# A two-block transformer kernel: wide products issued first, one memory projection left in float32, and mixers without GpSimd arithmetic

## The chip, the cores and the metric

The kernel runs on one core of one Trainium2 chip. A core has a matrix engine (TensorE, PE in the rows; PEld is its weight load), a vector engine (VectorE, DVE), an activation engine (ScalarE, ACT), GpSimd (POOL), and SyncE (SP), which here issues the loads. The metric is the device time of one execution in microseconds (us); lower is better.

## The reference

Two blocks of two layers each over one sequence of 256 tokens, width 1024, all in float32. Cut to what matters here:

```python
# block 1
x = x + attn_conv_mixer(rms_norm(x), ...);  x = x + swiglu(rms_norm(x), w_gate, w_up, w_down)     # d_ff 3584
x = x + recurrent_mixer(rms_norm(x), ...);  x = x + moe_swiglu(rms_norm(x), router, ...)          # 8 experts, top 2
# block 2, for l in (0, 1)
x = x + 0.5 * swiglu_2(rms_norm_2(x), ffn1...)                                                    # d_ff 2816
z = rms_norm_2(x) @ mix_w_in[l]
x = x + concat(fox_mixer(z_fox), rwkv7_mixer(z_rwkv), moba_mixer(z_moba)) @ mix_w_out[l]
x = x + memory_cross_attention(rms_norm_2(x), rms_norm_2(mem), ...)
x = x + 0.5 * swiglu_2(rms_norm_2(x), ffn2...)

def memory_cross_attention(h, m, w_q, w_kv, q_gain, k_gain, w_o):
    kv = (m @ w_kv)                  # 256 x 1024 @ 1024 x 1024: first half keys, second half values
    k, v = rms_norm_2(kv keys, k_gain), kv values
    ...                              # the memory side does not depend on x

def rwkv7_mixer(...):                # per token t, 8 heads of 64
    state = state * w_t + sa * (kk_t * a_t) + v_t * k_t;  y_t = state @ r_t
```

## The kernel before

Tokens lie on 256 columns, features on 128 partitions; a wide product has 512 columns. Products that must keep float32 accuracy are split: each weight tile of 128 x 1024 is copied by ACT into a rounded high part `wh` (L192) and DVE subtracts it to get the low part `wl` (L193); the activations have a high and a low part too, `msh`/`msl` or the two halves of `hTa`/`hTb`. A product is then three matmuls, `mm3` at L204 to L206 (high by high, high by low, low by high).

The stages run in the order hybrid, ffn0, lru, moe, f1_0, mix_0, xa_0, f2_0, f1_1, mix_1, xa_1, f2_1. In an FFN, gate and up go through `proj_wide` (L396, L397): since the high and low halves of the normed activations lie side by side in `n.both`, one matmul of 512 columns does two of the three, and one of 256 columns does `wl` by high. Eight such pairs (k = 0 to 7) make one group in one bank of PSUM, two groups each for gate and up make a chunk. The down product (`acc`) uses L204 to L206 with 512 columns.

Weights arrive by SP's queue in tiles of 1 MB (`wt`) in a ring of `RING` = 6 buffers, which also holds the normed activations `hTa`, `hTb`. Small tiles of 128 x 512 come from `w4`, a set of buffers of its own for each "lane"; `SLOTS` gives their numbers. A lane is a generator whose steps are put between those of the main work: `fill` advances lane "f" or "g" by so many steps. The order on each engine is the one in which the code issues after these fills, moved a little by the scheduler.

In lru, lane "f" is `memory(0)`: it norms the memory, projects keys (`pmk`, split) and values (`pmv`, split), and evicts the values to `xv` (L1135, ACT). `memory(1)` runs in xa_0. At the end of lru the moe stage starts: it issues five expert tiles ahead (`AHEAD`), then `route`: router logits `plg` (L211), top 2 on DVE down to `r_M` (L850), ranks `prk` (L858), the largest count `mosti` (L868). Then every engine loads `mosti` (L1017, TENSOR_LOAD), takes a branch together (L1018), and goes on with the gather by one-hot products `pxg` (L911, its lists `oneh` from DVE, L899) and the experts.

In the mixers the rwkv part works on chunks of 64 tokens. `key` gives k and its norm; `be` (the tiles `a`, L1396) and `f` (tiles `kf`, L1397) are products of 128 x 512 on GpSimd. DVE runs the reciprocal square roots (`rsqrt`, steps at L294 to L303, of which the last spreads the result to 128 x 512, `kksq`). `gram` (L1490 to L1495) forms the matrices `gN`, `gB`, `gM` of the chunks: ACT copies them out of PSUM (L1490), GpSimd clears what lies above the diagonal in two pieces (L1495). From `gN` a triangular inverse is built in five levels, each a product `pX` (L1529), an eviction, a product `pY` (L1537), and two DVE steps (L1538, L1539); lanes fill in between. `moba` turns q and k with `rot` (L1225) on PE and two GpSimd products each (L1228, L1229).

Of the kernel before, what the change touches and what calls it, by code (L numbers as in the profile page):

```python
# [14 lines left out]
P = 128  # L15
# [3 lines left out]
SLOTS = {"":19,"f":11,"g":14}  # L19
# [15 lines left out]
class Norm:  # L35
# [3 lines left out]
    def __init__(self, K, x, gcol, raw=False):  # L39
        self.K, self.gcol, self.raw = K, gcol, raw  # L40
        self.xv = x if callable(x) else lambda b, lo, hi: x[:, b, lo:hi]
        self.hT, self.both = [], []
        self.ss = K.work.tile([P, 2, 2], FT, name="ss", tag="ss", bufs=2)

    def half(self, half):
# [6 lines left out]
        for kk in range(2):  # L52
            if self.raw:
                hf = K.w4("hTf")
                self.hT += [hf[:, k * S:(k + 1) * S] for k in range(2)]
            pt = K.ps("pt", tag="acc")
            for j in range(2):
                k = half * 4 + kk * 2 + j
                for b in range(2):
                    nc.tensor.transpose(pt[:, j * S + b * P:j * S + (b + 1) * P], xv(b, k * P, (k + 1) * P), K.ident)  # L60
            for j in range(2):
                k = half * 4 + kk * 2 + j
                o, g, t = pt[:, j * S:(j + 1) * S], self.gcol[:, k:k + 1], self.hT[k]
                if self.raw:
                    nc.vector.tensor_scalar(t, o, g, None, op0=OP.mult)
                    continue
                nc.scalar.activation(t[0], o, AF.Identity, scale=g)
                nc.vector.scalar_tensor_tensor(t[1], o, g, t[0].bitcast(FT), op0=OP.mult, op1=OP.subtract)
# [42 lines left out]
class Kern:  # L111
    def __init__(self, ctx, tc, a):
        self.tc, self.nc, self.a = tc, tc.nc, a
        self.lane = ""
        self.kv, self.aside = {}, {}
# [274 lines left out]
    def proj_wide(self, t, j, n, name, tag):  # L390


        mm, o = self.nc.tensor.matmul, slice(j * P, (j + 1) * P)
        p = self.ps(name, tag=tag)
        for k in range(KT):
            mm(p, t[k][0][:, o], n.both[k], start=k == 0, stop=False)  # L396
            mm(p[:, :S], t[k][1][:, o], n.hT[k][0], start=False, stop=k == KT - 1)  # L397
        return self.v2(p)
# [331 lines left out]
    def lru(self, x):  # L730
# [16 lines left out]
        self.aside = {"f": self.memory(0) if "mem_2" in a else None, "g": gates()}  # L747
# [261 lines left out]
    def moe(self, x):  # L1009
        gcol = self.colA["norm_ffn1"]  # L1010
        n = Norm(self, x, gcol, raw=True)
        yield n
        ahead = [self.wfetch(self.a[("moe_w_gate", "moe_w_up")[i // 2 % 2]][0, 0], i % 2 * 4, 4, i // 4 * 512, 512)
                 for i in range(AHEAD)]
        self.route(x, n)
        ahead[:SPLIT] = [self.wsplit(t, 4, 512) for t in ahead[:SPLIT]]
# [10 lines left out]
    def block2_setup(self):  # L1027
# [27 lines left out]
        for i in (0, 2):  # L1055
            nc.vector.tensor_scalar(self.mask3[:, i], self.jp, 0.0, NEG, op0=OP.is_gt, op1=OP.mult)

# [46 lines left out]
    def memory(self, l):  # L1104
# [32 lines left out]
        self.kv[l] = kn, vs  # L1137

# [70 lines left out]
    def softmax_heads(self, l, hT, rbc, c0, qg, kg, rope, bias=None, extra=None, sums=None):  # L1209
# [7 lines left out]
        for i, g in enumerate((g8, kg)):  # L1217
# [5 lines left out]
            if rope:  # L1223
# [4 lines left out]
                nc.gpsimd.tensor_tensor(self.v2(q1), self.v2(q1), self.bc2(self.cos), op=OP.mult)  # L1228
                nc.gpsimd.tensor_tensor(q1, q1, t, op=OP.add)  # L1229
# [80 lines left out]
    def rwkv(self, l, hT, rbc, plo, pk0, done):  # L1310
# [77 lines left out]
        for tp in range(2):  # L1388
# [7 lines left out]
            nc.gpsimd.tensor_tensor(be, be, Wi[tp], op=OP.mult)  # L1396
            nc.gpsimd.tensor_tensor(f, f, k, op=OP.mult)  # L1397
# [78 lines left out]
        def gram(lst, i, name, also=None, tag="acc", lane=""):  # L1476

            res = []
            for tp in range(2):
# [10 lines left out]
                nc.scalar.activation(g, p, AF.Copy)  # L1490
                if also:
                    also(tp, p)
                g8 = g.rearrange("p (n s) -> p n s", n=8)
                for rows, base in ((P, 64), (64, 0)):
                    nc.gpsimd.affine_select(out=g8[:rows], in_=g8[:rows], compare_op=OP.is_ge if i else OP.is_gt, fill=0.0,  # L1495
                                            base=base, pattern=[[0, 8], [1, 64]], channel_multiplier=-1)
# [289 lines left out]
```

## Time and profile before

| | us |
|---|---|
| three runs | 2804.93, 2807.41, 2796.13 (median 2804.93) |
| profiled execution, its own time | 2807.59 |
| its span | 2804.8 |
| PE busy | 2728.8 (97% of the span) |
| DVE busy | 2087.6 (74%) |
| ACT busy | 1688.5 (60%) |
| POOL busy | 72.0 (3%), 121 instructions |
| mean granted clock of TensorE | 0.982 |

Times of rows count from the start of the span. "Busy" of PE is a modelled overlap: matmuls start before the ones ahead end, so the distance from start to start tells what one costs in a stream, not its duration. The clock column is the granted TensorE clock as a share of full speed: 1.0 is 2.4 GHz, 0.5 is 1.2 GHz. A row of waits names the engine that stood idle, its line, and the instruction that released it.

### The profile page before, as it was taken

Reading aid. Unit: us, or ns where it says so; the run is one execution under the profiler, and the core shown is the slowest. Engines: PE = TensorE matmul, PEld = TensorE weight load, DVE = VectorE, ACT = ScalarE, POOL = GpSimd, SP = SyncE. Lnnn points to the kernel's source line nnn. Section 1 sums busy time; section 2 is a strip of 40 time slices with the busy share of each in tenths; the row PEclk is TensorE's granted clock in tenths of the full one; section 3 lists DMA queues with packets and bytes.
Section 4 is the critical chain, followed back from the end, with each engine's and each line's share of the span. In section 5 each row is a group of like instructions: output and inputs, shape, how many; then the busy total and the mean of one; then the engine's idle time right before and its main releaser. Section 6 shows DMA issues by size and latency. Waiting matters only on the chain. (4 is left out here: it accounts for less than half of the span.)

```text
span 2804.8 us, 46759 instructions
## 1 busy us (share of the span) xinstructions
PE 2728.8 (97%) x18959; PEld 2289.3 (82%) x18959; DVE 2087.6 (74%) x3041; ACT 1688.5 (60%) x2380; POOL 72.0 (3%) x121
## 2 busy tenths in 40 slices
PE   8999988999999999999999999999999999998999
PEld 7888886878787778778778888788888888787887
DVE  7767677988888888889887667557666666766665
ACT  5555565777777777777776556345555555544554
POOL 0010000000000000000000001010000000110000
PEclk9999998999999999999999999799999999899999
DMA  5555535999999989999996554123555555232453
GB/s 182 182 196 183 179 106 186 344 345 366 323 370 351 369 307 365 357 337 358 348 366 227 186 172 126 61 77 121 190 186 180 191 184 177 61 107 91 137 193 105
DMA packets 355711, 623.55 MB, mean 222 GB/s; under 512 B 12580, under 2 KB 187952, under 8 KB 355488
## 3 DMA queue, kind: packets, MB, share of 16 engines
q1 hardware_dynamic: 354448, 620.20, 63.8%
q8 instruction: 150, 2.46, 0.4%
q0 software_dynamic: 1040, 0.29, 0.1%
q14 instruction: 73, 0.60, 0.1%
HBM read 619.40 MB, written 1.05 MB: 221 GB/s over the span
## 5 line engine op out<-in xcount | busy, mean ns | idle before, releaser
L193 DVE TENSOR_TENSOR wl<-wt,wh 128x1024 fp32r<-128x1024 f32 x1176 | 1389.7, 1219 | 371.4 <-ACT wh L192 369.6
L192 ACT ACTIVATE wh<-wt 128x1024 fp32r<-128x1024 f32 x1176 | 1187.6, 1052 | 434.6 <-PE acc L206 92.3
L204 PE MATMUL acc<-wh,msh 128*128 128x512 f32 x544 | 214.0, 394 | 0.0
L206 PE MATMUL acc<-wh,msl 128*128 128x512 f32 x544 | 213.3, 392 | 0.0
L205 PE MATMUL acc<-wl,msh 128*128 128x512 f32 x544 | 212.4, 390 | 0.0
L205 PE MATMUL pu<-wl,xgh 128*128 128x512 f32 x448 | 179.1, 400 | 3.7 <-DVE wl L193 3.7
L204 PE MATMUL pg<-wh,xgh 128*128 128x512 f32 x448 | 176.7, 395 | 1.3 <-ACT xgh L918 1.3
L205 PE MATMUL pg<-wl,xgh 128*128 128x512 f32 x448 | 177.7, 397 | 0.0
L205 PE MATMUL ya<-wl,eh 128*128 128x512 f32 x448 | 177.4, 400 | 0.0
L204 PE MATMUL pu<-wh,xgh 128*128 128x512 f32 x448 | 175.5, 392 | 0.0
L206 PE MATMUL pg<-wh,xgl 128*128 128x512 f32 x448 | 175.3, 391 | 0.0
L206 PE MATMUL pu<-wh,xgl 128*128 128x512 f32 x448 | 175.3, 391 | 0.0
L206 PE MATMUL ya<-wh,el 128*128 128x512 f32 x448 | 174.1, 393 | 0.0
L204 PE MATMUL ya<-wh,eh 128*128 128x512 f32 x448 | 162.1, 392 | 0.0
L396 PE MATMUL pu<-hTa,wh 128*128 128x512 f32 x424 | 155.2, 399 | 0.3 <-DVE rbc L88 0.3
L396 PE MATMUL pu<-hTb,wh 128*128 128x512 f32 x424 | 154.9, 399 | 0.0
L396 PE MATMUL pg<-hTa,wh 128*128 128x512 f32 x424 | 154.7, 399 | 0.0
L396 PE MATMUL pg<-hTb,wh 128*128 128x512 f32 x424 | 154.3, 398 | 0.0
L206 PEld LDWEIGHTS acc<-wh,msl 128*128 128x128 f32 x544 | 102.2, 188 | 23.9 <-DVE msl L511 1.3
L204 PEld LDWEIGHTS acc<-wh,msh 128*128 128x128 f32 x544 | 102.2, 188 | 21.6
L397 PE MATMUL pu<-hTa,wl 128*128 128x256 f32 x424 | 119.2, 281 | 0.6 <-DVE wl L193 0.6
L397 PE MATMUL pu<-hTb,wl 128*128 128x256 f32 x424 | 119.6, 282 | 0.0
(702 smaller groups left out, 5604.8 us busy)
## 6 DMA issues: line engine op xcount, KB each, us to landing
wt<-in_moe_w_gate SPq DMA_DIRECT2D x112, 1024.0 KB, 7.1
wt<-in_moe_w_up SPq DMA_DIRECT2D x112, 1024.0 KB, 7.3
wt<-in_moe_w_down SPq DMA_DIRECT2D x112, 1024.0 KB, 6.3
wt<-in_ffn_w_in SPq DMA_DIRECT2D x88, 1024.0 KB, 5.2
wt<-in_ffn_w_out SPq DMA_DIRECT2D x44, 1024.0 KB, 5.1
wt<-in_mix_w_in SPq DMA_DIRECT2D x24, 1024.0 KB, 5.8
wt<-in_ffn_w_gate SPq DMA_DIRECT2D x14, 1024.0 KB, 5.0
wt<-in_ffn_w_up SPq DMA_DIRECT2D x14, 1024.0 KB, 5.1
```

The source lines that it names most:

```text
L192: i = nc.scalar.activation(h[:, m], t[:, s], AF.Copy)
L193: j = nc.vector.tensor_tensor(lo[:, m], t[:, s], h.bitcast(FT)[:, m], op=OP.subtract)
L204: nc.tensor.matmul(out, l[0], r[0], start=first, stop=False)
L205: nc.tensor.matmul(out, l[0], r[1], start=False, stop=False)
L206: nc.tensor.matmul(out, l[1], r[0], start=False, stop=last)
L396: mm(p, t[k][0][:, o], n.both[k], start=k == 0, stop=False)
L397: mm(p[:, :S], t[k][1][:, o], n.hT[k][0], start=False, stop=k == KT - 1)
```

## The change

Five things. `proj_wide` issues the eight wide matmuls of a group first, then the eight narrow ones. `memory(0)` in lru is replaced by `memory_keys(0)`, which leaves the normed memory in float32 in one tile of the weight ring (`memT`) and multiplies float32 weights unsplit: 32 matmuls of 256 columns for the keys; the values are left for `memory_values`, 16 matmuls of 512 columns on two weight tiles (`held`) that are fetched at the start of moe and used inside `route`'s stretch, before the branch. Three of five expert tiles are issued ahead of `route`, two behind the values. In both mixers `be`, `f` and the two rope products go from GpSimd to DVE. A gram leaves PSUM by one DVE operation, a bitwise and with a mask `chunk` that is made once; the ACT copy and the GpSimd pieces are gone. `SLOTS[""]` goes from 19 to 18.

```diff
-SLOTS = {"":19,"f":11,"g":14}
+SLOTS = {"":18,"f":11,"g":14}
@@ Norm
-                hf = K.w4("hTf")
+                i = (2 * half + kk) * 512
+                hf = K.w4("hTf") if self.home is None else self.home[:, i:i + 512]
@@ proj_wide
         for k in range(KT):
             mm(p, t[k][0][:, o], n.both[k], start=k == 0, stop=False)
+        for k in range(KT):
             mm(p[:, :S], t[k][1][:, o], n.hT[k][0], start=False, stop=k == KT - 1)
@@ lru
-        self.aside = {"f": self.memory(0) if "mem_2" in a else None, "g": gates()}
+        self.aside = {"f": self.memory_keys(0) if "mem_2" in a else None, "g": gates()}
@@ moe
+        held = self.held and [self.wfetch(self.a["xattn_w_kv_2"][self.held[0]], 4 * kh, 4, 512, 512) for kh in range(2)]
         yield n
...
+        ahead = first(AHEAD - 2)
         self.route(x, n)
+        if held:
+            with self.on("f"):
+                self.memory_values(held)
+        ahead += first(AHEAD - 2, AHEAD)
@@ block2_setup
+        self.chunk = c.tile([P, 2, 64], I32, name="chunk")
+        cm = self.w4("chm", P).rearrange("p (i s) -> p i s", i=2)
+        for i, op in enumerate((OP.is_gt, OP.is_ge)):
+            for h in (slice(0, 64), slice(64, P)):
+                nc.vector.tensor_scalar(cm[h, i], self.jp[h, h], 0.0, -1.0, op0=op, op1=OP.mult)
+        nc.vector.tensor_copy(self.chunk, cm)
@@ new: memory_keys (norm as in memory, raw, home = a ring tile), its products
+            t = self.wfetch(wkv, 0, KT, pr * 256, 256)
+            p = self.ps("pmk")
+            for j in range(2):
+                for k in range(KT):
+                    nc.tensor.matmul(p[:, j * S:(j + 1) * S], t[:, k * 256 + j * P:k * 256 + (j + 1) * P], n.hT[k],
+                                     start=k == 0, stop=k == KT - 1)
+                    if k % 2:
+                        yield
@@ new: memory_values
+        pv = [self.ps("pmv") for _ in range(2)]
+        for k in range(KT):
+            for b in range(2):
+                nc.tensor.matmul(pv[b], n.hT[k][:, b * P:(b + 1) * P], t[k // 4][:, k % 4 * 512:(k % 4 + 1) * 512],
+                                 start=k == 0, stop=k == KT - 1)
+        for b in range(2):
+            v = self.w4("xv")
+            nc.scalar.activation(v, pv[b], AF.Identity, scale=n.r[:, b:b + 1])
@@ rope
-                nc.gpsimd.tensor_tensor(self.v2(q1), self.v2(q1), self.bc2(self.cos), op=OP.mult)
-                nc.gpsimd.tensor_tensor(q1, q1, t, op=OP.add)
+                nc.vector.tensor_tensor(self.v2(q1), self.v2(q1), self.bc2(self.cos), op=OP.mult)
+                nc.vector.tensor_tensor(q1, q1, t, op=OP.add)
@@ rwkv
-            nc.gpsimd.tensor_tensor(be, be, Wi[tp], op=OP.mult)
-            nc.gpsimd.tensor_tensor(f, f, k, op=OP.mult)
+            V.tensor_tensor(be, be, Wi[tp], op=OP.mult)
+            V.tensor_tensor(f, f, k, op=OP.mult)
@@ gram
-                nc.scalar.activation(g, p, AF.Copy)
                 if also:
                     also(tp, p)
-                g8 = g.rearrange("p (n s) -> p n s", n=8)
-                for rows, base in ((P, 64), (64, 0)):
-                    nc.gpsimd.affine_select(out=g8[:rows], in_=g8[:rows], compare_op=OP.is_ge if i else OP.is_gt, fill=0.0,
-                                            base=base, pattern=[[0, 8], [1, 64]], channel_multiplier=-1)
+                bits = lambda t_: t_.bitcast(I32).rearrange("p (n s) -> p n s", n=8)
+                V.tensor_tensor(bits(g), bits(p), self.chunk[:, i:i + 1, :].to_broadcast([P, 8, 64]), op=OP.bitwise_and)
```

How the order moves at three places. First, PE from the last transposes of moe's norm (`pt`) to the branch, before:

```order
L211 MATMUL plg<-wr,hTf 32x8 x20
L60 MATMUL pt<-ident,x 128x128 x6
L211 MATMUL plg<-wr,hTf 32x8 x32
L858 MATMUL prk<-r_M,before 128x16
L858 MATMUL prk<-r_M,ones 128x16
L1017 TENSOR_LOAD mosti
L1018 COMPARE_AND_BRANCH
```

The same place of PE now, where lines count two or three higher, and L1194 is the matmul of `memory_values`:

```order
L213 MATMUL plg<-wr,hTf 32x8 x20
L1194 MATMUL pmv<-wt,memT 128x512
L62 MATMUL pt<-ident,x 128x128 x6
L1194 MATMUL pmv<-wt,memT 128x512
L213 MATMUL plg<-wr,hTf 32x8 x24
L1194 MATMUL pmv<-wt,memT 128x512
L213 MATMUL plg<-wr,hTf 32x8 x8
L1194 MATMUL pmv<-wt,memT 128x512 x5
L861 MATMUL prk<-r_M,before 128x16
L861 MATMUL prk<-r_M,ones 128x16
L1194 MATMUL pmv<-wt,memT 128x512 x8
L1029 TENSOR_LOAD mosti
```

Three of the sixteen stand ahead of the last router product, five ahead of `prk`, eight between `prk` and the load that the branch needs. On ACT, the activations at the same place, before:

```order
L875 ACTIVATE xsh<-x,rstd 128x512 x4
L845 ACT_TABLE_LOAD
L845 ACTIVATE r_e<-r_e 128x2
L1017 TENSOR_LOAD mosti
L1018 COMPARE_AND_BRANCH
```

And ACT now:

```order
L878 ACTIVATE xsh<-x,rstd 128x512 x4
L848 ACT_TABLE_LOAD
L848 ACTIVATE r_e<-r_e 128x2
L1199 ACTIVATE xv<-pmv,rstd 128x512 x2
L1029 TENSOR_LOAD mosti
L1030 COMPARE_AND_BRANCH
```

The two evictions of the values, which need all sixteen matmuls, have come ahead of ACT's own load and branch. Second, DVE in mixer 0, at the first of the two keys, before (`nwt`, `nwg` are the steps of a reciprocal square root, `wl` a weight split):

```order
L193 TENSOR_TENSOR wl<-wt,wh 128x1024
L298 TENSOR_TENSOR nwt<-nwt 128x8
L294 TENSOR_SCALAR nwg<-hn_t 128x8
L1269 COPY fz<-fz 4x256
L299 SCALAR_TENSOR_TENSOR nwt<-nwt,hn_t 128x8
L295 TENSOR_TENSOR nwg<-magic,nwg 128x8
L1407 TENSOR_TENSOR cum<-kf,cum 128x512
L303 SCALAR_TENSOR_TENSOR kksq<-nwt 128x512
```

DVE there now:

```order
L195 TENSOR_TENSOR wl<-wt,wh 128x1024
L300 TENSOR_TENSOR nwt<-nwt 128x8
L296 TENSOR_SCALAR nwg<-hn_t 128x8
L1461 TENSOR_TENSOR a_24269<-a_24269,cum 128x512
L301 SCALAR_TENSOR_TENSOR nwt<-nwt,hn_t 128x8
L297 TENSOR_TENSOR nwg<-magic,nwg 128x8
L1462 TENSOR_TENSOR kf<-kf,k 128x512
L305 SCALAR_TENSOR_TENSOR kksq<-nwt 128x512
L300 TENSOR_TENSOR nwt<-nwg 128x8
L1472 TENSOR_TENSOR cum<-kf,cum 128x512
```

`be` (L1461) and `f` (L1462) now stand on DVE ahead of the spread `kksq` that PE waits for, and the copy of `fz` and the product `cum` have gone behind it.

Third, PE in mixer 0 ahead of the inverse's first products, where the narrow matmuls `pv` of a lane stand between `gN` and `pX`. Before, `pX` came after 38 of them, of which these are the last:

```order
L597 MATMUL tm<-ident,av 128x128 x2
L205 MATMUL pv<-hTa,wh 128x256
L1272 MATMUL pct<-ident,fz 128x4 x2
L206 MATMUL pv<-hTa,wl 128x256
L204 MATMUL pv<-hTa,wh 128x256
L205 MATMUL pv<-hTa,wh 128x256
L1529 MATMUL pX<-TI,gN 32x32 x45
L463 MATMUL hn<-ident,hn_sq 128x128 x4
L1529 MATMUL pX<-TI,gN 32x32 x19
L1537 MATMUL pY<-X,T_24654 32x32 x64
```

PE there now, from the second `gN` on (the rows left out are the rest of twelve `pv`):

```order
L1551 MATMUL gN<-ar,a_24275 64x64 x16
L1487 MATMUL hw<-ident,v 64x64 x16
L206 MATMUL pv<-hTa,wh 128x256
...
L1591 MATMUL pX<-TI,gN 32x32 x32
L206 MATMUL pv<-hTb,wh 128x256
L207 MATMUL pv<-hTb,wh 128x256
L1591 MATMUL pX<-TI,gN 32x32 x32
L1599 MATMUL pY<-X,T_24524 32x32 x64
```

Twelve `pv` are left between the second `gN` and the first `pX`; most of the others have gone behind the first `pY`.

## Rows read from the trace of the kernel before

**Rows 1.** Stages: stretch, length, busy PE, PEld, DVE, ACT, POOL, clock, DMA share, GB/s.

```profile
350.00:469.00 119.00, 109.24 (x806) 100.08 (x807) 92.57 (x168) 72.34 (x118) 0.81 (x16) 0.96 0.46 162
469.00:492.00 23.00, 11.33 (x162) 9.05 (x151) 15.55 (x58) 11.66 (x17) 0.00 (x0) 0.64 0.24 83
...
1689.00:1912.30 223.30, 211.66 (x3268) 178.35 (x3267) 139.67 (x308) 105.84 (x209) 25.11 (x26) 0.92 0.26 81
...
2356.20:2568.40 212.20, 205.09 (x3268) 174.32 (x3267) 139.41 (x306) 106.09 (x209) 24.49 (x26) 0.96 0.30 95
```

**Rows 2.** Page, part 5: a narrow group; busy us, mean ns, idle before it.

```profile
L397 PE MATMUL pu<-hTa,wl 128*128 128x256 f32 x424 | 119.2, 281 | 0.6 <-DVE wl L193 0.6
```

**Rows 3.** Timeline of PE in an FFN chunk: start, duration, line, tiles, shapes.

```profile
1600.16 0.40 PE L396 MATMUL pg<-hTb,wh 128*128 128x512 f32 x1
1600.40 0.28 PE L397 MATMUL pg<-hTb,wl 128*128 128x256 f32 x1
...
1601.93 0.40 PE L396 MATMUL pg<-hTa,wh 128*128 128x512 f32 x1
```

**Rows 4.** Timeline of PE in an FFN down product, three starts ten matmuls apart.

```profile
1609.70 0.40 PE L204 MATMUL acc<-wh,msh 128*128 128x512 f32 x1
...
1612.03 0.39 PE L205 MATMUL acc<-wl,msh 128*128 128x512 f32 x1
...
1614.30 0.39 PE L206 MATMUL acc<-wh,msl 128*128 128x512 f32 x1
```

**Rows 5.** Timeline of PE in the mixers and xa_0: split, then unsplit float32.

```profile
1724.79 0.28 PE L204 MATMUL pqk<-hTa,wh 128*128 128x256 f32 x1
1724.91 0.28 PE L205 MATMUL pqk<-hTa,wh 128*128 128x256 f32 x1
...
1809.13 1.13 PE L1442 MATMUL pbn<-r,bones 128*128 128x512 f32 x2
...
1887.11 1.98 PE L1647 MATMUL pmean<-gy,bones 128*128 128x512 f32 x4
...
1928.42 1.03 PE L1164 MATMUL xsp<-xk,xq 128*128 128x256 f32 x4
```

**Rows 6.** PE's waits, 380 to 492 us: total, times, longest.

```profile
PE pxg L911 <- DVE oneh L899: 6.0, 1, 6.0
PE prk L858 <- DVE r_M L850: 4.7, 1, 4.7
PE pmk L204 <- ACT wh L192: 3.0, 1, 3.0
```

**Rows 7.** Timeline of ACT behind the route's branch; brackets: idle before.

```profile
483.51 1.28 ACT L192 ACT_TABLE_LOAD   x1 [5.36 <-SPq L1018]
```

**Rows 8.** Groups of POOL: count, busy us, mean ns.

```profile
L1396 POOL TENSOR_TENSOR a<-a,cum 128x512 f32<-128x512 f32 x4 | 6.2, 1560 | 1812.8 <-ACT kf L1393 1812.6
```

**Rows 9.** Timeline of DVE in mixer 0 while POOL works on L1396.

```profile
1735.77 1.28 DVE L299 SCALAR_TENSOR_TENSOR nwt<-nwt,hn_t 128x8 f32<-128x8 f32 x1
...
1737.05 1.75 DVE L1407 TENSOR_TENSOR cum<-kf,cum 128x512 f32<-128x512 f32 x1
```

**Rows 10.** Source view of L1326: ns min/median/max, first and last start.

```profile
L1326 DVE TENSOR_TENSOR vz<-pv,rbc x4: 692/692/692, 1731.1 to 2440.3; 128x512 f32<-128x512 f32 x4
```

**Rows 11.** PE's waits in mixer 0, then (last row) mixer 1.

```profile
PE hn L463 <- DVE kksq L303: 4.2, 1, 4.2
PE pX L1529 <- issue: 2.3, 1, 2.3
PE pY L1537 <- issue: 2.2, 1, 2.2
...
PE hn L463 <- DVE kksq L303: 2.9, 1, 2.9
```

**Rows 12.** Stretches inside the mixers, columns as in Rows 1.

```profile
1762.50:1793.20 30.70, 28.43 (x449) 19.77 (x438) 13.91 (x42) 8.45 (x26) 0.53 (x1) 0.50 0.12 36
...
2400.00:2440.00 40.00, 35.20 (x645) 30.05 (x645) 28.80 (x65) 15.60 (x37) 9.25 (x8) 0.79 0.18 53
```

More of the change, by code (lines that the diff above doesn't have):

```diff
@@ L35, with __init__ @@
 class Norm:
-    def __init__(self, K, x, gcol, raw=False):
-        self.K, self.gcol, self.raw = K, gcol, raw
+    def __init__(self, K, x, gcol, raw=False, home=None):
+        self.K, self.gcol, self.raw, self.home = K, gcol, raw, home
         self.xv = x if callable(x) else lambda b, lo, hi: x[:, b, lo:hi]
@@ L114, in __init__ @@
         self.lane = ""
-        self.kv, self.aside = {}, {}
+        self.kv, self.aside, self.held = {}, {}, None
         self.table, self.others = None, []
@@ L1011, in moe, with first @@
         n = Norm(self, x, gcol, raw=True)
+        held = self.held and [self.wfetch(self.a["xattn_w_kv_2"][self.held[0]], 4 * kh, 4, 512, 512) for kh in range(2)]
         yield n
-        ahead = [self.wfetch(self.a[("moe_w_gate", "moe_w_up")[i // 2 % 2]][0, 0], i % 2 * 4, 4, i // 4 * 512, 512)
-                 for i in range(AHEAD)]
+        def first(*r):
+            return [self.wfetch(self.a[("moe_w_gate", "moe_w_up")[i // 2 % 2]][0, 0], i % 2 * 4, 4, i // 4 * 512, 512)
+                    for i in range(*r)]
+        ahead = first(AHEAD - 2)
         self.route(x, n)
+        if held:
+            with self.on("f"):
+                self.memory_values(held)
+        ahead += first(AHEAD - 2, AHEAD)
         ahead[:SPLIT] = [self.wsplit(t, 4, 512) for t in ahead[:SPLIT]]
@@ L1137, in memory, with memory_keys, memory_values @@
         self.kv[l] = kn, vs
+    def memory_keys(self, l):
+        nc, a, C = self.nc, self.a, self.colB
+        wkv = a["xattn_w_kv_2"][l]
+        mt = self.ring.tile([P, 2048], FT, name="mem", tag="ring").rearrange("p (b d) -> p b d", b=2)
+        nc.sync.dma_start(mt, a["mem_2"][0].rearrange("(b p) d -> p b d", p=P))
+        n = Norm(self, mt, C[f"mem_norm{l}"], raw=True, home=self.ring.tile([P, 2048], FT, name="memT", tag="ring"))
+        for half in range(2):
+            n.half(half)
+            yield
+        n.stats()
+        n.rows()
+        kn = []
+        for pr in range(2):
+            t = self.wfetch(wkv, 0, KT, pr * 256, 256)
[5 more added lines that the diff above has]
+                    if k % 2:
+                        yield
+            k1 = self.w4("xk")
+            nc.vector.tensor_tensor(self.v2(k1), self.v2(p), self.bc2(n.rbc), op=OP.mult)
+            rk = self.headnorm(k1, 2, P)
+            nc.vector.scalar_tensor_tensor(k1, k1, C[f"xk_gain{l}"], rk, op0=OP.mult, op1=OP.mult)
+            kn.append(k1)
+        self.held = l, n, kn
+    def memory_values(self, t):
+        nc = self.nc
+        l, n, kn = self.held
+        pv = [self.ps("pmv") for _ in range(2)]
[3 more added lines that the diff above has]
+                                 start=k == 0, stop=k == KT - 1)
+        vs = []
+        for b in range(2):
+            v = self.w4("xv")
+            nc.scalar.activation(v, pv[b], AF.Identity, scale=n.r[:, b:b + 1])
+            vs.append(v)
+        self.kv[l] = kn, vs
+        self.held = None
     def xattn(self, x, l):
```

## The prediction

> **What bounds the kernel now.** I read the engine shares first: PE is busy for 97% of the span, so a change counts only where it shortens PE's stream, ends one of its waits, or lifts its clock. Then a table by stage: the FFN stages and the experts have next to no idle PE, while lru idles for 119.0 − 109.24 = 9.8 us, the route for 11.7 us at a mean clock of 0.64, mixer 0 for 11.6 us and mixer 1 for 7.1 us [rows 1]. Mixer 0 takes 223.3 us and mixer 1, the same code, 212.2: clock 0.92 against 0.96 and 4.5 us of idle time tell them apart. Then, stage by stage, PE's waits and the timeline. In the FFN the low weights are no wait: 0.6 us over 424 narrow matmuls [rows 2].
>
> **Wide first in `proj_wide`.** Five pairs take 1601.93 − 1600.16 = 1.77 us, 0.354 each, of which 0.24 belongs to the wide one and 0.115 to the narrow one [rows 3]. The wait for `wl` is worth nothing, so the edit can gain only by the pitch of like matmuls in a row. In a down product, which follows such pairs, the first ten wide ones take 0.233 each and the next ten 0.227 [rows 4]; narrow ones in a row keep 0.12 [rows 5]. A group of eight and eight is 8 × 0.354 = 2.83 us now; at 0.233 and 0.12 it would be 2.82, at 0.227 and 0.12 2.78, so 8 to 56 ns less. There are 424 × 4 wide matmuls in all, so 212 groups: 2 to 12 us. I take **−4**, near the low end, because a group is only eight long and the down product needed ten; the range is 0 to −12.
> By a rule this would be nothing: the Trainium skill ("TensorE: Matmul & The Clock Gate", section "Back-to-back issue gap") gives the distance of two matmuls at full clock by the columns alone, 512/2.4 + 2.5 and 256/2.4 + 2.5 ns, an estimate of 325 ns a pair in any order, where the rows show 354. With it the sum below would be 4 us higher.
>
> **Memory in lru.** Keys: before, 96 narrow split matmuls at 0.12 = 11.5 us [rows 5]. An unsplit float32 matmul runs as two instructions: four instructions of 256 columns take 1.03 us with their tail, and for 512 columns four take 1.98 where two take 1.13, so one matmul costs 0.85 in a stream, and one of 256 columns half of it, 0.43 [rows 5]. Now 32 × 0.43 = 13.8, 2.3 more. Values: before 48 split wide ones at 0.23 = 11.1 us, which leave the stage. PE's work in lru falls by 8.8 us. The wait of `pmk` for the split `wh`, 3.0 us [rows 6], loses the split but keeps the load ahead of it; eight weight splits each on ACT and DVE go, which also feed the other 6.8 us of idle. I take 3 of 9.8 us. Sum **−12**, from −6 (idle time grows by 3) to −18 (nearly all goes).
>
> **Values in the route.** Sixteen matmuls of 512 columns at 0.85 are 13.6 us. Cover is there: PE idles for 4.7 us ahead of `prk`, and 6.0 ahead of `pxg` [rows 6]. But the order decides. The five that stand between the last `plg` and `prk`, with those three among the router products, take 6.8 us for an idle time of 4.7, so `prk` comes some 1.2 us later (part of the three runs in the pauses between router products). Eight more, 6.8 us, stand behind `prk`. Then ACT's two evictions, about 0.7 each as for a DVE eviction of that shape [rows 10], must end before ACT reaches the branch. Before, ACT stood at the branch from 483.51 − 5.36 = 478.15 and waited for the others [rows 7]; they were held by `mosti`, which DVE makes from `prk`. Now ACT comes at 478.2 + 1.2 + 6.8 + 0.7, about 487. This is the **new wait**: behind it on ACT are the first weight splits, behind the branch on DVE the lists `oneh`, and PE waits for both. The branch itself and the `pxg` stretch follow unchanged. Price 0 to +9; I take **+7**, since no other engine can enter the branch's fetch early. The half clock of the stretch stays: PE still idles behind the branch. On SP the two value tiles go ahead of the expert tiles, and the last two of these five wait for ring buffers (the fifth for one that the value products free) ahead of SP's own load; SP is then through before ACT. They land while the branch and `pxg` run; without that cover up to +6, two waits such as `pmk`'s 3.0 [rows 6], which I hold as a tail.
> Together lru and route: −5.
>
> **Mixers.** POOL works 25.1 and 24.5 us in them [rows 1], hardly on PE's path by itself, but DVE crawls beside it: `cum` takes 1.75 us and a step of the square root on 8 elements a partition 1.28 [rows 9], where 512 elements take 0.69 [rows 10]; both lie inside POOL's products of some 1.56 us [rows 8]. On PE's path lies the wait of `hn` for the spread `kksq`: 4.2 us in mixer 0, 2.9 in mixer 1 [rows 11]. Now two products, 1.4 us, stand ahead of that spread, in place of 1.28 + 1.75 and two more steps slowed like the first; `cum` has gone behind. The wait falls to about 1: a gain of 3 and 2. The half clock follows such idle time: in mixer 1 the clock is 0.79 over the 40 us around that wait [rows 12]. The big piece is the stretch from 1762.5, 30.7 us at 0.50 [rows 12], behind waits of 2.2 and 2.3 us in the chain `pX`, `pY` [rows 11]; at full clock PE's 28.4 busy us would be about 14. Mixer 1 ran the same chain without it, so it hangs on small pauses; I give it an even chance, −7.
> Against it: DVE takes on 16 operations of 0.69 a mixer, 11 us (four for `be`, `f`, four for rope, eight grams) [rows 10]. In the inverse the gram is masked by DVE behind a `copy_predicated` and an eviction, and PE now has 12 narrow matmuls, 1.4 us, between `gN` and the first `pX`, where it had 38, 4.6 us. That costs 0 to 4 us a mixer; I take 3. ACT loses eight copies, off the path. Rope and the later grams have lane products queued on PE and count nothing; uncovered, four operations of 0.69, 3 us.
> Mixer 0: −3 − 1 − 7 + 3 = **−8** (−22 to +6). Mixer 1: −2 − 5 + 3 = **−4** (−9 to +5). The one mask in ffn0 and the slot fewer: nothing, behind a full PE.
>
> **Sum.** −4 − 12 + 7 − 8 − 4 = −21 from 2807.6, the profiled execution's own time, of which the span is 2804.8. That execution is 2.7 above the median of the three runs, which spread over 11 us. Forecast 2787.
>
> **Rivals.**
> (1) *The cover is lost as fast as it is found.* Lru gives only 9, the route's wait costs the full 8 to 9, the FFN gives 3, and the mixers nothing, DVE's new work taking the place of the slowed steps. 2807.6 − 3 − 9 + 8.5 = 2804. For it: the evictions before the branch. Against it: the slowed DVE rows.
> (2) *The inverse starves and the half clock takes both mixers.* With the filling matmuls spent early, PE pauses at `pX` and `pY` in mixer 1 as it did in mixer 0. From pauses of about 4.5 us together (2.3 + 2.2) the 30.7 us stretch came; it costs 14 us, now in mixer 1 as well, with 3 to 4 us of waits in each while mixer 0 keeps its own stretch: −4 − 12 + 7 + 3 + 18 = +12, **2820**, slower. Against it: mixer 1 has escaped so far.
> (3) *All goes at once.* The wide stream settles immediately (−11), mixer 0 loses the long half-clock stretch altogether and comes to what mixer 1 takes less a few (−20), mixer 1 gives 6: −11 − 12 + 7 − 20 − 6 = −42, **2766**.
> (4) *The order of wide and narrow makes no difference.* The cost follows the columns, whatever is ahead, and the rest is as forecast: 2791. For it: a narrow one costs 0.12 in both streams [rows 3, 5]; against it: wide ones at 0.227 in the long stream [rows 4]. This is what the rule of the Trainium skill named above gives.
>
> **How the numbers follow.** Forecast 0.35, (1) 0.27, (2) 0.10, (3) 0.16, (4) 0.12. About 0.5%, 14 us, is what a measurement can tell from no change: faster is below 2791, slower above 2819. The forecast's own spread is 2776 to 2798, most of it faster (0.30); with all of (3), half of (4) and a little of (1), faster has 0.55. Slower is over half of (2) and tails of (1): 0.08. Same is the rest, 0.37. The range leaves out (2) and the lower half of (3): 2762 to 2812.
>
> **What would show it.** In the FFN: wide starts nearer to 0.227 than 0.24 late in a group of eight (right), or pairs that still cost 0.354 in sum ((4)). In lru no `wh` ahead of `pmk`, and a stage of about 107 us. In the route ACT's idle time before the branch gone, and the first expert matmul at about 7 us more behind the last `plg`; if the branch comes as early as before, my new wait is wrong. In the mixers no DVE step of eight columns over 0.2 us, the wait of `hn` near 1, and the stretch behind the first `pX` at full clock. A half-clock stretch of 30 us in both mixers would make the forecast wrong, and so would experts that wait for loads.

## The result, and the profile after

The changed kernel takes 2775.94 us (median of 4 runs, 2774.46 to 2776.51), the kernel before 2806.17 (median of 4, 2796.13 to 2808.66): ratio 0.9896, 95% interval 0.9877 to 0.9916. It is **faster by 1.0%**; the forecast was 2787, the range 2762 to 2812. In later comparisons the kernel before had medians of 2800.6 to 2804.4 with single runs from 2794 to 2811, while the changed one came again at 2776.24: some 24 to 28 us are the change, the rest of the 30 is where the first four runs of before fell.

The first line of the page's part on engines, for the changed kernel (busy time, share, instructions):

```profile
PE 2713.7 (98%) x18911; PEld 2278.1 (82%) x18911; DVE 2067.2 (75%) x3070; ACT 1652.3 (60%) x2348; POOL 24.2 (1%) x73
```

PE's busy time has fallen by 15 us and its idle time by as much. The spans are 2804.8 and 2774.7. Cut at the first transpose of each stage's norm (and at `prk`, the first `pxg` and the first expert product in the route), the two traces differ so; the lengths are differences of start times:

| stretch | before | after | difference | forecast |
|---|---|---|---|---|
| ffn0, f1_0, f2_0, f1_1, f2_1 | 998.2 | 988.2 | −10.0 | −4 |
| lru | 118.7 | 106.3 | −12.4 | −12 |
| first router transpose to `prk` | 10.8 | 12.3 | +1.5 | |
| `prk` to first `pxg` | 7.0 | 11.3 | +4.3 | |
| `pxg` to first expert product | 4.9 | 5.1 | +0.2 | route +7 in all |
| mixer 0 | 223.3 | 211.9 | −11.4 | −8 |
| mixer 1 | 212.1 | 210.3 | −1.9 | −4 |
| experts, hybrid, xa_0, xa_1 | 1224.7 | 1224.3 | −0.4 | 0 |

The rows of the changed kernel that answer to [rows 1], by stretch: length, busy PE, PEld, DVE, ACT and POOL with instructions, clock, DMA share, GB/s. First lru, then the route up to `prk`, the route from `prk`, mixer 0, mixer 1:

```profile
345.80:452.00 106.20, 98.66 (x703) 89.12 (x702) 81.66 (x156) 60.72 (x103) 0.94 (x16) 0.97 0.53 178
452.00:464.30 12.30, 12.30 (x167) 7.12 (x166) 8.92 (x37) 5.43 (x11) 0.00 (x0) 1.00 0.01 3
464.30:480.80 16.50, 11.98 (x38) 6.95 (x36) 6.22 (x22) 7.45 (x11) 0.00 (x0) 0.84 0.49 166
1674.40:1886.30 211.90, 204.18 (x3268) 173.53 (x3267) 140.88 (x323) 101.60 (x201) 0.99 (x2) 0.96 0.27 83
2327.00:2537.30 210.30, 204.18 (x3267) 173.47 (x3266) 140.48 (x321) 101.53 (x201) 1.01 (x2) 0.96 0.29 94
```

Up to `prk` the route has no idle PE any more, and behind it 4.5 us; mixer 0 has 7.7 us of idle time where it had 11.6, and its clock has risen from 0.92 to 0.96. The two mixers now look alike.

The timeline of PE in an FFN of the changed kernel, beside [rows 3, 4] (start, duration, line, tiles, shapes, count; a row joins the matmuls of one kind, and the view ends inside the last one):

```profile
1587.08 1.07 PE L398 MATMUL pg<-hTa,wh 128*128 128x512 f32 x4
1587.98 1.07 PE L398 MATMUL pg<-hTb,wh 128*128 128x512 f32 x4
1588.89 0.64 PE L400 MATMUL pg<-hTa,wl 128*128 128x256 f32 x4
1589.36 0.64 PE L400 MATMUL pg<-hTb,wl 128*128 128x256 f32 x4
1589.84 1.09 PE L398 MATMUL pg<-hTa,wh 128*128 128x512 f32 x4
1590.77 1.07 PE L398 MATMUL pg<-hTb,wh 128*128 128x512 f32 x4
1591.68 0.52 PE L400 MATMUL pg<-hTa,wl 128*128 128x256 f32 x3
```

The first group follows a down product, a long row of wide matmuls: its wide ones take 0.90 + 0.91 us, 0.226 each, from the first on. The second group follows eight narrow ones: its first four take 0.93, the next four 0.91. In the medians over the 140 groups of eight that follow narrow ones, the starts of the wide ones lie 0.233, 0.236, 0.228, 0.232, 0.231, 0.227, 0.227 and 0.227 apart, and the narrow ones 0.113 once and then 0.120. Such a group takes 2.79 us where eight pairs took 2.83; the 49 that follow a down product, one in four, take 2.77.

PE's waits in the changed kernel's lru and route (us in total, times, longest), beside [rows 6]:

```profile
PE acc L207 <- DVE wl L195: 5.1, 1, 5.1
PE pxg L914 <- DVE oneh L902: 3.9, 1, 3.9
```

The waits of `prk` and `pmk` are gone. In their place stands one that no step of the prediction had: 5.1 us of lru's output product `acc` for the low half of its first weight tile, at 424 us. The route's own new wait is on ACT; its timeline, beside [rows 7]:

```profile
464.55 0.20 ACT L848 ACTIVATE r_e<-r_e 128x2 f32<-128x2 f32 x1
470.96 0.69 ACT L1199 ACTIVATE xv<-pmv,rstd 128x512 f32<-128x512 f32 x1 [6.20 <-PE pmv L1194]
471.81 0.69 ACT L1199 ACTIVATE xv<-pmv,rstd 128x512 f32<-128x512 f32 x1 [0.17 <-PE pmv L1194]
475.16 1.28 ACT L194 ACT_TABLE_LOAD   x1 [2.66 <-ACTq L1030]
```

ACT stands for 6.20 us for the values and evicts them until 472.50; its load of `mosti` and its branch come at 471.8 and 472.3, some 8 us behind `prk`. The others did not wait for it at the branch. DVE's own load and ACT's (in the order: duration min/median/max in ns, first and last start), and DVE's first step behind the branch:

```profile
L1029 DVEq TENSOR_LOAD <-mosti x1: 547/547/547, 466.3 to 466.3; - x1
L1029 ACTq TENSOR_LOAD <-mosti x1: 464/464/464, 471.8 to 471.8; - x1
475.01 0.87 DVE L902 TENSOR_SCALAR oneh<-iota,r_rk 128x128 fp32r<-128x128 f32 x4 [8.50 <-ACTq L1030]
```

PE, GpSimd and SyncE load at 465.6 to 465.7. So the branch is not taken together, as it nearly was before (all five loads at 479.0 to 479.7); what waits for ACT is the work behind it. What PE does in that time:

```profile
459.90 4.56 PE L1194 MATMUL pmv<-wt,memT 128*128 128x512 f32 x10
464.30 0.29 PE L861 MATMUL prk<-r_M,before 128*128 128x16 f32 x2
464.44 0.37 PE L861 MATMUL prk<-r_M,ones 128*128 128x16 f32 x2
464.67 7.11 PE L1194 MATMUL pmv<-wt,memT 128*128 128x512 f32 x16
475.63 0.75 PE L914 MATMUL pxg<-oneh,xsh 128*128 128x256 f32 x2 [3.86 <-DVE oneh L902]
```

Five values' products (ten instructions) end as `prk` starts, 0.7 us after its input `r_M` is ready; eight more run for 7.11 us behind it.

DVE in mixer 0 of the changed kernel, at the key of [rows 9]:

```profile
1721.03 0.69 DVE L1461 TENSOR_TENSOR a<-a,cum 128x512 f32<-128x512 f32 x1
1721.63 0.16 DVE L301 SCALAR_TENSOR_TENSOR nwt<-nwt,hn_t 128x8 f32<-128x8 f32 x1
...
1721.79 0.68 DVE L1462 TENSOR_TENSOR kf<-kf,k 128x512 f32<-128x512 f32 x1
1722.39 0.69 DVE L305 SCALAR_TENSOR_TENSOR kksq<-nwt 128x512 f32<-128x512 f32 x1
...
1723.07 0.68 DVE L1472 TENSOR_TENSOR cum<-kf,cum 128x512 f32<-128x512 f32 x1
```

The step L301 (L299 before) takes 0.16 us where it took 1.28, and `cum` 0.68 where it took 1.75; no step of eight columns in either mixer takes more than 0.18. The two products themselves take 0.69 and 0.68 on DVE; POOL had taken 1.56 for `be` [rows 8] and 1.28 for `f` on the mean. PE's waits in mixer 0 now, beside [rows 11]:

```profile
PE pY L1599 <- issue: 2.6, 1, 2.6
PE pX L1591 <- issue: 1.8, 1, 1.8
PE hn L213 <- ACT hn_sq L428: 1.2, 1, 1.2
PE gN L1551 <- DVE a L1470: 1.1, 1, 1.1
```

The wait of `hn` for `kksq` has left the list; a shorter one, of `gN` for `a`, has come. The pauses of the inverse, 2.6 and 1.8, have stayed.

### The profile page after: what moved, and what is told of

The parts are those of the page before. It is cut to its first block, busy times and chain, and to the rows that moved or that the text cites. A ratio compares the mean times of both kernels' runs of the same rounds, so it can differ in the third digit from the quotient of the medians.

```text
span 2774.7 us, 46450 instructions
## 1 busy us (share of the span) xinstructions
PE 2713.7 (98%) x18911; PEld 2278.1 (82%) x18911; DVE 2067.2 (75%) x3070; ACT 1652.3 (60%) x2348; POOL 24.2 (1%) x73
## 5 line engine op out<-in xcount | busy, mean ns | idle before, releaser
L195 DVE TENSOR_TENSOR wl<-wt,wh 128x1024 fp32r<-128x1024 f32 (+1 forms) x1168 | 1377.9, 1217 | 352.8 <-ACT wh L194 215.4
L194 ACT ACTIVATE wh<-wt 128x1024 fp32r<-128x1024 f32 (+1 forms) x1168 | 1168.8, 1050 | 413.4 <-issue 106.5
L207 PEld LDWEIGHTS acc<-wl,msh 128*128 128x128 f32 x544 | 103.1, 189 | 24.6 <-DVE wl L195 5.4
L398 PE MATMUL pu<-hTa,wh 128*128 128x512 f32 x424 | 117.5, 395 | 0.0
L398 PE MATMUL pg<-hTa,wh 128*128 128x512 f32 x424 | 115.1, 393 | 0.2 <-DVE ft L495 0.2
L398 PE MATMUL pu<-hTb,wh 128*128 128x512 f32 x424 | 114.5, 390 | 0.0
L398 PE MATMUL pg<-hTb,wh 128*128 128x512 f32 x424 | 113.6, 390 | 0.0
L207 PEld LDWEIGHTS pu<-wl,xgh 128*128 128x128 f32 x448 | 84.1, 188 | 32.7 <-DVE wl L195 15.8
```

The source lines that it names most:

```text
L194: i = nc.scalar.activation(h[:, m], t[:, s], AF.Copy)
L195: j = nc.vector.tensor_tensor(lo[:, m], t[:, s], h.bitcast(FT)[:, m], op=OP.subtract)
L207: nc.tensor.matmul(out, l[0], r[1], start=False, stop=False)
```

## The experiments

Three theories were on trial beside the forecast's terms: that each part brings alone what it brings in the whole; that the mixers gain because DVE is no longer held up by GpSimd, not because of the grams; and that what the values cost in the route is the eight products behind `prk`.

**Wide first alone.** The kernel before, with this edit:

```diff
             mm(p, t[k][0][:, o], n.both[k], start=k == 0, stop=False)
+        for k in range(KT):
             mm(p[:, :S], t[k][1][:, o], n.hT[k][0], start=False, stop=k == KT - 1)
```

> The kernel before with one edit: the eight wide products of a group ahead of the eight narrow ones. Theory: the shorter FFN stages of the changed kernel (2.2, 2.7, 1.6, 1.6 and 1.8 us, 10 in all) come from this edit alone, so the five FFN stages lose 9 to 10 us and no other stage moves by more than the swing that mixer 0 shows from run to run; in a group the wide starts come down from 0.236 to 0.227 us by the sixth, and the narrow ones stand at 0.120. Rival (order makes no difference, the FFN gained by something else in the change): under 3 us, pairs still cost 0.354.

Measured 2794.49 us (8 runs), ratio 0.9971 (0.9955 to 0.9987). The five FFN stages lose 2.3, 1.8, 1.7, 1.6 and 1.8 us, 9.2 together; f1_1 goes from 187.8 to 186.1. No other stage moves by more than 1.2 us except the mixers and the experts (−1.8); the mixers also swing between runs of one kernel. The theory holds, and the order does make a difference.

**Memory alone.** The kernel before with `memory_keys`, `memory_values` and what they need, as in the diff of the change, and nothing else of it.

```diff
-        self.aside = {"f": self.memory(0) if "mem_2" in a else None, "g": gates()}
+        self.aside = {"f": self.memory_keys(0) if "mem_2" in a else None, "g": gates()}
...
+        if held:
+            with self.on("f"):
+                self.memory_values(held)
```

> The kernel before with the memory change alone: keys unsplit in lru, values unsplit ahead of the branch. Theory (new wait): lru 12 us shorter, the stretch from the first router transpose to the first expert product 6 us longer, sum -6; ACT idles some 6 us for pmv ahead of its branch. Rival (the lru gain in the changed kernel comes in part from the other edits): lru shorter by under 8 us, sum 0.

Measured 2796.76 (10 runs), ratio 0.9978 (0.9967 to 0.9988). Lru takes 105.9 us, 12.8 less; from the first router transpose to the first expert product it is 28.9 us where it was 22.8, 6.1 more. ACT's timeline there:

```profile
473.23 0.69 ACT L1191 ACTIVATE xv<-pmv,rstd 128x512 f32<-128x512 f32 x1 [6.20 <-PE pmv L1186]
```

The same 6.20 us. Both terms stand by themselves, −12.8 + 6.1.

**The mixers alone, and their two halves.** Three kernels, each the kernel before with part of the mixers' change. The first has all of it:

```diff
+            V.tensor_tensor(be, be, Wi[tp], op=OP.mult)
+            V.tensor_tensor(f, f, k, op=OP.mult)
...
+                nc.vector.tensor_tensor(q1, q1, t, op=OP.add)
...
+                V.tensor_tensor(bits(g), bits(p), self.chunk[:, i:i + 1, :].to_broadcast([P, 8, 64]), op=OP.bitwise_and)
```

> The kernel before with GpSimd out of the mixers (four products, rope, grams). Theory: mixer 0 falls by 8 to 12 us and mixer 1 by 2, no DVE step of 8 columns takes over 0.2 us, the wait of hn for kksq is gone, and the 30 us stretch at half clock in mixer 0 does not come. Rival (that stretch comes and goes by chance and the edit removes only the wait of hn): mixer 0 falls by 3 to 5, the stretch stands in some run as before, mean gain 5.

The second has the last line of these alone:

> The kernel before with the grams alone changed: masked by one DVE operation as they leave PSUM; the four products be and f and the rope stay on GpSimd. Theory (DVE is held up by the GpSimd products at the two keys, and the grams matter little): the wait of hn of 4.2 and 2.9 us stays, gain under 3 us. Rival (the grams' copy and mask on two engines were what held the inverse): mixer 0 falls by 8 or more although that wait stays.

The third has `be`, `f` and rope on DVE, and the grams as before:

> The kernel before with be, f and the rope products on DVE, the grams still copied by ACT and cleared by GpSimd. Theory (DVE held up by the GpSimd products is what cost the mixers): the wait of hn for kksq falls from 4.2 and 2.9 to under 0.5 us, mixer 0 stands at 208 to 214 us and mixer 1 at 209 to 211, gain 8 to 10, as much as with the grams too. Rival (it is the two together, the grams by GpSimd still make PE pause in the inverse): the 24 to 37 us at half clock in mixer 0 come as before, gain under 5.

| | median us | ratio to before (95%) | mixer 0 | mixer 1 |
|---|---|---|---|---|
| all | 2793.28 (10 runs) | 0.9967 (0.9955 to 0.9979) | 208.6 | 209.5 |
| grams alone | 2807.14 (10 runs) | 1.0010 (0.9998 to 1.0023) | 215.5 | 219.7 |
| products alone | 2796.04 (10 runs) | 0.9967 (0.9956 to 0.9977) | 211.8 | 210.5 |

Each comes out by its theory: with all of it the wait of `hn` is gone and mixer 0 stands 10 us under the mean of the four traces with GpSimd's products; the grams gain nothing; the products gain 8.4 us. So the products bring all of the gain that can be told; rope moved together with `be` and `f`, and which of them counts was not run apart. With the grams alone the wait that the products end still stands, in mixer 1 as long as in mixer 0. Grams alone, PE's waits of mixer 1, and the mixer's row:

```profile
PE hn L463 <- DVE kksq L303: 4.2, 1, 4.2
PE pY L1541 <- issue: 2.5, 1, 2.5
...
2349.10:2568.80 219.70, 210.89 (x3268) 178.50 (x3267) 142.18 (x313) 101.53 (x201) 13.36 (x10) 0.93 0.28 88
```

Products alone, PE's waits of mixer 0: the wait for `kksq` is gone although ACT and POOL still do the grams.

```profile
PE pX L1529 <- issue: 2.1, 1, 2.1
PE pX L1529 <- DVE TI L1516: 1.5, 2, 1.0
PE hn L211 <- ACT hn_sq L425: 1.2, 1, 1.2
PE gN L1486 <- DVE a L1405: 1.1, 1, 1.1
```

**The changed kernel again**, beside the next three on one chip.

> The changed kernel itself, unedited, beside the next three. Both theories: 2776, 27 us under the kernel before as measured on the same chip; mixer 0 between 208 and 213 us, since no 30 us stretch at half clock comes in it.

Measured 2776.24 (4 runs), ratio 0.9909 (0.9875 to 0.9942), mixers 209.5 and 210.6.

**The low half earlier in lru.** The changed kernel, with its new wait of 5.1 us attacked:

```diff
-        parts = []
+        parts = []; w0 = self.wload(wo, 0, 2, 0, D)
...
-            parts.append(([[u[:, TS(j)] for u in y] for j in range(2)], lambda pr=pr: self.wload(wo, 2 * pr, 2, 0, D)))
+            parts.append(([[u[:, TS(j)] for u in y] for j in range(2)], lambda pr=pr: self.wload(wo, 2 * pr, 2, 0, D) if pr else w0))
```

> The changed kernel with the first weight tile of lru's output product split ahead of the scans, so that its low half wl no longer stands behind them on DVE. Theory: the new wait of 5.1 us of acc for that wl is a matter of DVE's order alone; it falls to about 1, the half-clock stretch behind it goes, lru is 5 to 7 us shorter, the rest unchanged. Rival (DVE is the bound at the end of lru, whatever its order): PE waits as long for the products msl of the last scans, lru within 1 us.

Measured 2770.69 (4 runs), ratio 0.9892 (0.9858 to 0.9925). Lru takes 103.4 us where it took 106.8 in the kernel beside it: 3.5 less, between the two theories. What PE waits for now (two of the rows):

```profile
PE acc L206 <- DVE xk L1183: 1.8, 1, 1.8
PE hn L466 <- DVE hn_t L305: 1.4, 1, 1.4
```

The order was the cause of the 5.1 us, but other work of DVE at the end of lru, the norm of the second keys, holds PE next: 3.2 us of waits stand where 5.1 stood. PE's idle time in lru falls by 2.5 us; the granted clock of the stage is 0.98 where it was 0.97.

**Sixteen wide, then sixteen narrow.** The changed kernel; two groups, in two banks, go together:

```diff
...
+        for j in range(2):
+            for k in range(KT):
+                mm(p[j], t[k][0][:, j * P:(j + 1) * P], n.both[k], start=k == 0, stop=False)
+        for j in range(2):
+            for k in range(KT):
+                mm(p[j][:, :S], t[k][1][:, j * P:(j + 1) * P], n.hT[k][0], start=False, stop=k == KT - 1)
...
```

> The changed kernel with sixteen wide products (two groups in two banks) ahead of sixteen narrow ones. Theory (what costs is the passage from narrow to wide: six wide starts that come down from 0.236 to 0.227, some 30 ns a group): half of the passages go, 106 of 212, so the FFN stages lose 2 to 4 us in all. Rival (the pitch depends on the bank or the eviction, not on the run's length): no change, or a loss where the eviction of the first bank comes later.

Measured 2774.13 (4 runs), ratio 0.9907 (0.9873 to 0.9941): not to be told from the changed kernel by its time. By stage, f2_0, f1_1 and f2_1 lose 0.36 us each, and ffn0 gains 0.7, of which 0.6 is a wait of its own:

```profile
PE pg L396 <- DVE colC L262: 0.6, 1, 0.6
```

The direction is the theory's, the size is half of it: 0.36 us for the 22 passages from narrow to wide that go in such a stage, some 17 ns each.

**Half of the values in lru.** The changed kernel; the first eight of the values' products run in lane "f" behind the keys, are evicted, and the route adds the other half:

```diff
+        t = self.wfetch(wkv, 0, 4, 512, 512)
+        pv = [self.ps("pmv") for _ in range(2)]
+        for k in range(4):
+            for b in range(2):
+                nc.tensor.matmul(pv[b], n.hT[k][:, b * P:(b + 1) * P], t[:, k * 512:(k + 1) * 512], start=k == 0, stop=k == 3)
+                yield
...
+            nc.vector.scalar_tensor_tensor(vs[b], pv[b], n.r[:, b:b + 1], vs[b], op0=OP.mult, op1=OP.add)
```

> The changed kernel with half of the values' sixteen products done in lru, evicted and added later, so that eight are left in the route, all ahead of prk. Theory (the route's new wait is the eight products behind prk, and the idle time of 5.1 us in lru can cover the other eight): PE and ACT come to the branch right behind prk, the stretch from prk to the first expert product falls by 6 us, lru grows by 2, sum -4 or better. Rival (the branch is held by something else, or lru's idle time is not open to these products): route falls by under 2 or lru grows by 7, sum 0 or more.

Measured 2769.25 (4 runs), ratio 0.9891 (0.9856 to 0.9925). PE at lru's end and in the route:

```profile
422.12 3.70 PE L1189 MATMUL pmv<-wt,memT 128*128 128x512 f32 x8
425.26 1.03 PE L206 MATMUL acc<-wh,msh 128*128 128x512 f32 x2
426.60 2.84 PE L1189 MATMUL pmv<-wt,memT 128*128 128x512 f32 x6 [0.31 <-ACT xv L1194]
...
464.40 0.37 PE L861 MATMUL prk<-r_M,before 128*128 128x16 f32 x2 [0.16 <-DVE r_M L853]
...
471.28 0.77 PE L914 MATMUL pxg<-oneh,xsh 128*128 128x256 f32 x2 [6.30 <-DVE oneh L902]
```

And DVE's first step behind the branch:

```profile
470.65 0.87 DVE L902 TENSOR_SCALAR oneh<-iota,r_rk 128x128 fp32r<-128x128 f32 x4 [4.52 <-DVEq L1030]
```

No product stands behind `prk` now, DVE goes on from its own branch and not from ACT's, and the first `pxg` comes 6.9 us after `prk`, as in the kernel before (7.0), in place of 11.3: 4.4 less. Lru, with eight products more, is 106.4 us, 0.4 less than beside it: they fill the wait of `acc`, and lru's granted clock is 1.00 where it was 0.97:

```profile
345.40:451.80 106.40, 103.18 (x719) 90.30 (x718) 81.70 (x156) 62.31 (x105) 0.94 (x16) 1.00 0.55 187
```

**Both later edits, and again.** Half of the values in lru with sixteen wide in every FFN:

> The changed kernel with both later edits: half of the values in lru, and sixteen wide ahead of sixteen narrow. Theory: they touch different stages and add up, -6 and -1 against the changed kernel, 2768 to 2770. Rival (no gain from the second, or one that mixer states swallow): 2769 or above, not to be told from half of the values alone.

Measured 2772.71 (5 runs), ratio 0.9902 (0.9883 to 0.9921): above the theory's 2768 to 2770, as the rival has it. Then half of the values alone, once more, and with sixteen wide in the four FFN stages of block 2 only (`if F < 3584`), both on one chip:

> The changed kernel with half of the values in lru, once more, beside the next one on the same chip. Theory: 2769 to 2771, 6 us under the changed kernel's 2776. Rival (the first measurement fell on fast mixers): 2774 or more.

> The same with sixteen wide ahead of sixteen narrow in the four FFN stages of block 2 alone; ffn0, where a group so ordered waited 0.6 us for the columns colC that the hooked setup makes on DVE, keeps groups of eight. Theory: each of the four stages 0.35 us shorter, 1.4 us in all, with no loss in ffn0. Rival: the sum is not to be told from half of the values alone.

Measured 2773.56 (5 runs), ratio 0.9905 (0.9886 to 0.9923), which is above the theory's 2771 and just under the rival's 2774, and 2774.44 (4 runs), 0.9897 (0.9877 to 0.9917), where the rival holds. By stage half of the values repeats itself: `prk` to `pxg` 7.1 us, lru 106.4. In the last one the four FFN stages are each 0.35 shorter and ffn0 is as in groups of eight, as expected; but its profiled execution has mixer 0 so:

```profile
1670.70:1886.80 216.10, 209.14 (x3267) 177.31 (x3266) 140.80 (x323) 101.58 (x201) 0.99 (x2) 0.93 0.26 81
```

That is 4 us more than the others at a clock of 0.93, with the same code in the mixer. So an edit of 1 to 5 us is read from its stage here, not from the kernel's time. By its stages, lru and the route, half of the values in lru is worth 4.0 to 4.8 us against the two traces of the changed kernel. By time it is 7 us ahead on the one chip where both ran, 2769.3 against 2776.2; by the ratios to the kernel before, 0.9891 and 0.9905 against 0.9896 and 0.9909, it can't be told from the changed kernel. No clear gain by time was left for the sixteen.

## Why the prediction was right, point by point

**Sign, size and place of the sum.** Forecast −21, measured −30 in the profiled pair and −24 to −28 against the later medians of before. Every stage's sum has the sign that it was given.

**Wide first: the term that was mis-sized.** −4 was forecast, within 0 to −12; −10.0 and −9.2 were measured, and −9.0 in the second trace of the changed kernel. The step that failed is "near the low end, because a group is only eight long and the down product needed ten". The ten were read from a down product that followed alternating pairs. Behind eight narrow ones the pitch is down to 0.227 by the sixth wide start, narrow ones keep 0.120, and the group saves 39 ns; one group in four follows a down product instead, stands at 0.227 from its first start, and saves some 65. Over 212 groups that is 9.7 us, where 19 ns each had been taken. Rival (4), no difference, falls by the kernel with that edit alone. With it the rule of the Trainium skill that was named ("TensorE: Matmul & The Clock Gate", section "Back-to-back issue gap") does not describe this stream: 2.79 against 2.83 us for the same columns in another order. That section gives the formula for matmuls in isolation and says that weight loads count too in a real stream, which the prediction did not say.

**Lru: −12 forecast, −12.4 and −12.8 measured.** PE's busy time in it fell by some 10 us and its idle time by 2.2, close to 8.8 and 3; part of the 10 is less half clock (0.96 to 0.97). `pmk` waits no more. What was not seen is the new wait of 5.1 us at lru's end, in a stage where DVE is 77% busy. It is in the kernel with memory alone too, so it comes from that part; the idle time that the prediction had counted as 9.8 less 3 was in part exchanged for another, and that the sum of 3 came out near is luck.

**Route: +7 forecast, +6.0 and +6.1 measured.** The steps were `prk` 1.2 later, eight products of 6.8 us (7.11 with their tail) and the evictions on ACT ahead of the branch, as the rows of ACT show. `prk` comes 1.5 later: the three products among the router's put `r_M` back by 0.9, and the five behind them end 0.6 too late. One reason given was wrong: "no other engine can enter the branch's fetch early". They all did, DVE 5.5 us ahead of ACT; what held PE is that the lists wait for ACT to come out. The size was off by one: DVE takes up its lists 2.5 us after ACT's last eviction, where before it took 3.7 from its own last step. Half of the values in lru bears the mechanism out: without products behind `prk` and without evictions on ACT the stretch is back at 6.9. It took both away at once, so products and evictions are not told apart.

**Mixers: −8 and −4 forecast, −11.4 and −1.9 in the pair.** A pair of traces is a poor measure here. Four kernels of this study keep the GpSimd products (before, wide first, memory, grams) and ten have them on DVE; by their traces mixer 0 takes 218.9 us on the mean (215.5 to 223.3) against 211.5 (208.6 to 216.2), mixer 1 214.3 (211.6 to 219.7) against 210.2 (208.4 to 212.7): **−7.4 and −4.1**. The first step, that DVE is held up beside POOL and `hn` waits for it, is shown: the step of 1.28 us takes 0.16, the wait is gone, in the kernel with the products alone as in the changed one. The forecast left 1 us of that wait; 1.1 came at `gN`. In the same means PE's idle time falls by 3.1 us in mixer 0 and 2.6 in mixer 1, where −3 and −2 were forecast.

The other terms did not come as forecast. Half clock was to give 8 us in mixer 0 (1 and 7) and 5 in mixer 1, and the inverse to take 3 in each; the 1 and the 5 were taken without a working. PE's busy time falls by 4.2 and 1.5 us. By the granted clock of the traces mixer 0 runs at half clock for 37.5, 30.7, 23.9 and 23.9 us in the four kernels, and for 13.7 to 20.5 in the ten but for one with 30.7 (the last experiment); mixer 1 for 17.9 on the mean of four and 16.4 of ten. One stretch of 30 us stands in the kernel before alone; the 30.7 us of the last experiment have one of 23.9, and the 30.7 us in mixer 1 of the grams alone (clock 0.93) none over 10.3. Behind the first `pX` of the changed kernel's mixer 0 two stretches of 6.8 us are left, not none. What makes them long in one execution and short in the next was not settled. The price of 3 us for the inverse did not show in mixer 0: its pauses, 2.6 and 1.8 us, are what they were, 2.2 and 2.3. In mixer 1 they are 2.9 us in sum where they were 1.6. So the sums of −8 and −4 agree with −7.4 and −4.1 in part by luck: two terms of opposite sign were each too large.

**Rivals.** (1), 2804, needed the FFN to give 3 and the mixers nothing. (2), 2820, came nearest in one trace of the grams alone, where mixer 1 took 219.7 us, but with the wait of `hn` and in short stretches; it is not in the changed kernel. (3), 2766, was right on the FFN and not on the mixers.

**Hidden edits.** The expert tiles issued later cost nothing: the experts take 1007.3 us against 1008.5. The one mask and the slot fewer show nowhere.

## What to carry to other kernels

Before an arithmetic operation is left on GpSimd because GpSimd is idle, look at what DVE's short steps take beside it: here the price was on DVE, up to eight times the step's length, and PE waited for that. When work is moved into another stage's idle time, count how much of it stands ahead of the instruction that ends the idle time and how much behind: eight products ahead of `prk` cost 1.5 us, eight behind it 4.4 until they went elsewhere. Where two runs of the same code differ by 10 us, read an edit's worth from the stage it touches, in several traces.

## What the runs showed of the hardware that was not expected

A short DVE step beside a GpSimd product does not run slowly through it, it ends when the product ends. The product beside the step of 1.28 us in [rows 9], which ends at 1737.05:

```profile
1735.77 1.26 POOL L1396 TENSOR_TENSOR a<-a,cum 128x512 f32<-128x512 f32 x1 [0.17 <-ACT kf L1393]
```

All 16 steps of eight columns that take over 1 us, in the four traces with GpSimd's products, end 19 to 27 ns after the GpSimd product that ran beside them. So what such a step costs is what is left of that product. `cum`, of 512 columns, ends 0.55 us behind the next product. That every kind of DVE instruction is held so is not shown.

A wide matmul that follows narrow ones costs more than one in a row of wide ones: 0.233 and 0.236 us for the first two, 0.227 from the sixth on, at full granted clock throughout (f1_1: clock 1.00, no idle PE). A stream that alternates takes 0.354 us a pair, against 0.347 for the two kinds apart. A passage from narrow to wide costs some 27 ns (a group of 2.793 us behind narrow ones, of 2.766 behind a down product), and some 7 come back at the passage to narrow, where the first takes 0.113 and not 0.120; the sixteen wide, with one passage of each kind less, saved 17. Why was not found.

A bitwise and on DVE that reads PSUM and writes SBUF needs no more than a product of the same shape. The source view of the mask's line in the changed kernel (durations min/median/max in ns):

```profile
L1558 DVE TENSOR_TENSOR gM<-gM,chunk x8: 681/686/692, 1853.5 to 2509.0; 128x512 int32<-128x512 int32 x8
```

Sixteen such operations replaced sixteen ACT copies and thirty-two GpSimd pieces at no loss that can be told, and no gain.
